# Probabilities times values of the 64 wide heads: three fp32r products of split operands, or one native fp32 product in two column groups of the array

## The chip, the cores and the metric

One NeuronCore of a Trainium2 chip runs the whole program. The metric is the device time of one execution in microseconds (us); lower is better. TensorE (PE in the rows) does matrix products and transposes, VectorE (DVE), ScalarE (ACT) and GpSimd (POOL) the element-wise work, SyncE (SP) issues the DMA transfers. TensorE runs at one of two clock levels, 1.2 or 2.4 GHz; the rows give the granted clock as a share of 2.4 GHz.

## The reference, cut to what matters

The model is two residual layers and a second block, in float32, on 1024 tokens and 256 context tokens of 1024 features. Three of its attentions have heads of 64 features, and only these are touched by the change. Each ends in a product of probabilities and values:

```python
# even layer, windowed heads: 8 heads, 2 of keys and values, 128 queries a block
p = _sink_probs([s_loc, s_ctx], sink).astype(v.dtype)
return (jnp.einsum('bkgqs,bskd->bqkgd', p[..., :span], vn)
        + jnp.einsum('bkgqc,bckd->bqkgd', p[..., span:span + L], vc))
...
# odd layer, neighbourhood heads: 8 heads, 8 rows of the grid and the context
return (jnp.einsum('bhqk,bkhd->bqhd', p[..., :n_loc], vs)
        + jnp.einsum('bhqc,bchd->bqhd', p[..., n_loc:], vc))
...
# second block, dilated heads: 8 heads, causal; three windows, mixed by their denominators
o = jnp.einsum('nbqk,nbkd->nbqd', e, vb) / den[..., None]
```

The other two attentions (differential heads, low-rank heads) have values of 128 features and stay as they are.

## The kernel before, in words

The kernel keeps float32 accuracy with the faster fp32r products by splitting an operand into two fp32r parts, high and low, whose sum is the float32 value. A product of two split operands is three matmuls: high by high, low by high, high by low (lines 236 to 238, `mm3`, for the projections).

The program is a row of stages. In three of them an attention with 64 wide heads is woven with other work: `unit_a` (windowed heads, about 300 to 580 us of the span) with projections, `unit_d` (neighbourhood heads, about 1625 to 1930 us) with gates and half of the output projection, `unit_s` (dilated heads, about 2420 to 2680 us) with gates, a gated unit and half of the output projection. `woven` (line 485) takes steps from two generators so that their TensorE times, as the program notes them, advance in proportion; within an attention `pipe` (line 509) lets later parts of one unit go beside the first parts of the next. Engines run their instructions in program order, so TensorE does what the weave wrote, attention and other work in turns.

A unit has four steps. `front` makes scores of 128 queries (matmuls), their maximum (DVE, line 192), the exponential (ACT) and the division by the denominator (POOL). `back` transposes the probabilities, 128 by 128, on TensorE into a PSUM tile `ps_w`; `pt_evac` (lines 748 to 751) then takes the tile out of PSUM in two: ACT writes the high part, rounded to fp32r, and DVE subtracts it from PSUM to get the low part. The transposed tiles are `a_t`, `d_t` and `d_x` (neighbourhood and context keys), `s_th` and `s_tl`. `end` walks over key tiles of 128 and calls `pv64` (line 871) for each:

```python
    if not first:
        mm(o[0:64, cs], v[:, 0, :], lo, start=False, stop=False)                 # L875
    mm(o[:, cs], v.rearrange("p a e -> p (a e)"), hi, start=first, stop=last)    # L876
    if first:
        mm(o[0:64, cs], v[:, 0, :], lo, start=False, stop=False)                 # L878
```

The values stand in a row as 64 high and 64 low columns. One matmul with 128 stationary columns gives high values by high probabilities in PSUM rows 0 to 63 and low values by high probabilities in rows 64 to 127; a second with 64 columns adds high values by low probabilities. Up to 512 columns stream through, for the windowed heads 4 heads of 128 queries, for the others 4 query tiles of one head; a key tile that only some of the queries see has 384, 256 or 128 columns. `fold` (line 754) adds the two halves: ACT copies rows 64 to 127 out (`fo_a`), DVE adds rows 0 to 63 (`fo_b`), and a DMA writes the rows of y.

The values come from `kv_finish` (windowed) and `v_tok` (the others), which split them (ACT and DVE, lines 198 and 199) and spill 128 columns for a head to DRAM; `vals` loads them for each head.

In all there are 84 calls of `pv64` in the windowed stage (all of 512 columns), 128 in the neighbourhood stage (each of its 16 units: five of 512 columns and one each of 384, 256 and 128) and 96 in the dilated stage (8 units of 512, 384, 256 and 128 columns, 8 units with four of 512 more), 308 in all, and so 616 matmuls.

Another place matters for reading the trace: the state space part of the second block (`ssm`, line 1704) has native fp32 matmuls of 128 rows and 64 columns already, 16 in a row, in turn to PSUM rows 0 to 63 and 64 to 127, and lines 1743 and 1745 have native fp32 matmuls of other shapes.

Of the kernel before, what the change touches and what calls it, by code (L numbers as in the profile page):

```python
# [104 lines left out]
class Kern:  # L105
# [168 lines left out]
class Stream:  # L274
    """split weights one after the other, the next on its way; specs: (src [kc*P, n], how to split or None)"""
# [64 lines left out]
class Slabs:  # L340
    """tiles [k][c] of n columns each, indexed as one [:, k, a:b]"""
# [10 lines left out]
def cols(pair, a, b):  # L352
    """columns a..b of a split operand, by contraction tile"""
# [9 lines left out]
def tlast(n):  # L363
    """groups of tokens, the smaller one first"""
# [3 lines left out]
def cond_silu(K):  # L368
    """silu of c and c_ctx as columns [P, KD, 2]"""
# [419 lines left out]
def unit_a(K, ap, g, n, qd, hd, mask, yd):  # L789
# [1868 lines left out]
```

## Time and profile before

| | |
|---|---|
| device time, median of 3 runs (lowest, highest) | 2860.63 us (2854.64, 2862.84) |
| span of the profiled execution, first to last instruction | 2852.8 us |
| what lies around the span | not listed; the median is 7.8 us above this span |
| PE busy | 2508.2 us, 88% of the span |
| DVE, ACT, POOL busy | 61%, 41%, 30% |
| mean granted clock of TensorE | 0.94 |

The profiled execution's own device time stands in none of the views; the difference of 7.8 us between its span and the median of the runs is taken for what lies around it. A busy PE is no full PE: the ends of matmuls are modelled and overlap the next ones, so how long the engine is taken by one instruction is read from the start of one to the start of the next.

### The profile page before, as it was taken

What the parts mean: (1) busy time and instruction counts of PE and PEld (TensorE: products, weight loads), DVE (VectorE), ACT (ScalarE), POOL (GpSimd) and SP (SyncE); (2) the same over time, 40 slices, a digit from 0 to 9 for tenths busy, and PEclk for the clock granted to TensorE, in tenths of its full rate; (3) what the DMA queues carried; (4) which work ended last, traced back from release to release, by engine and by line L of the source; (5) the groups of instructions that cost most, each with busy time, mean ns of one, the idle gap of its engine ahead of it and who ended that gap; (6) DMA issues with size and microseconds to landing.
All of it is one profiled execution on the core that took longest, in us unless ns stands there. A gap on an engine that the chain in (4) does not pass through costs nothing.

```text
span 2852.8 us, 41862 instructions
## 1 busy us (share of the span) xinstructions
PE 2508.2 (88%) x14199; PEld 2124.0 (74%) x14199; DVE 1747.4 (61%) x5069; ACT 1173.1 (41%) x2589; POOL 868.6 (30%) x1149
## 2 busy tenths in 40 slices
PE   6687889779998977969999899897997889999998
PEld 4567777668977766947988777675996778877777
DVE  7552567557898976434555566668427774667643
ACT  6321455434454533323333355544213332555522
POOL 4231344300034444122232343452013442224410
PEclk9899999889999989989999999999998989999999
DMA  6235433243366443266332454665212224358521
GB/s 224 85 126 165 125 94 86 56 135 111 79 209 208 146 143 127 82 204 244 115 123 100 125 132 113 189 188 174 81 35 61 66 72 151 111 152 249 181 80 44
DMA packets 325496, 370.15 MB, mean 130 GB/s; under 512 B 39596, under 2 KB 258712, under 8 KB 325282
## 3 DMA queue, kind: packets, MB, share of 16 engines
q1 hardware_dynamic: 325122, 367.42, 42.4%
q8 instruction: 113, 1.85, 0.3%
q14 instruction: 101, 0.83, 0.1%
q10 hardware_dynamic: 160, 0.05, 0.0%
HBM read 240.49 MB, written 126.91 MB: 129 GB/s over the span
## 4 chain that ended last, share of the span: by engine, by line
PE 58%; DVE 17%; DMA 14%; POOL 4%; ACT 4%; issue 3%; SPq 1%; DVEq 0%; ACTq 0%; POOLq 0%
PE ps_w L236 11%; PE ps_w L238 10%; PE ps_w L237 10%; PE ps_w L894 4%; PE ps_w L904 3%; PE ps_w L876 2%; PE ps_w L1437 1%; PE ps_w L875 1%; PE ps_s L238 1%; PE ps_s L236 1%; PE ps_s L237 1%; PE ps_w L917 1%; PE ps_w L915 1%; PE ps_w L916 1%; DVE wl L215 1%
## 5 line engine op out<-in xcount | busy, mean ns | idle before, releaser
L215 POOL TENSOR_TENSOR wl<-raw,wh 128x256 fp32r<-128x256 f32 (+1 forms) x266 | 214.5, 822 | 534.2 <-ACT wh L210 384.6
L210 ACT CAST wh<-raw 128x256 fp32r<-128x256 f32 (+1 forms) x430 | 151.6, 402 | 139.3 <-PE ps_w L237 95.1
L215 DVE TENSOR_TENSOR wl<-raw,wh 128x256 fp32r<-128x256 f32 x220 | 128.0, 609 | 123.8 <-ACT wh L210 119.5
L236 PE MATMUL ps_w<-wo_h,o_yh 128*128 128x512 f32 x416 | 177.7, 427 | 15.3 <-ACT o_yh L198 10.1
L236 PE MATMUL ps_w<-e_hh,wh 128*128 128x512 f32 (+1 forms) x480 | 180.9, 377 | 7.0 <-DVE va_t L199 6.7
L238 PE MATMUL ps_w<-wo_h,o_yl 128*128 128x512 f32 x416 | 171.6, 413 | 12.1 <-DVE o_yl L199 12.1
L238 PE MATMUL ps_w<-e_hh,wl 128*128 128x512 f32 (+1 forms) x480 | 174.6, 364 | 5.5 <-DVE wl L215 5.5
L237 PE MATMUL ps_w<-e_hl,wh 128*128 128x512 f32 (+1 forms) x480 | 174.5, 364 | 0.0
L237 PE MATMUL ps_w<-wo_l,o_yh 128*128 128x512 f32 x416 | 170.2, 409 | 0.0
L236 PE MATMUL ps_w<-wh,s_hh 128*128 128x256 f32 x512 | 165.7, 324 | 0.0
L237 PE MATMUL ps_w<-wl,s_hh 128*128 128x256 f32 x512 | 162.7, 318 | 0.0
L238 PE MATMUL ps_w<-wh,s_hl 128*128 128x256 f32 x512 | 162.6, 318 | 0.0
L192 DVE CUSTOM_DVE_ANT_0 b_p<-ps_w,zero 128x512 f32<-128x512 f32 (+1 forms) x192 | 109.5, 593 | 27.8 <-PE ps_w L894 27.6
L236 PE MATMUL ps_w<-o_hh,wh 128*128 128x512 f32 (+1 forms) x288 | 114.9, 399 | 8.1 <-ACT wh L210 7.1
L236 PEld LDWEIGHTS ps_w<-wh,s_hh 128*128 128x128 f32 x512 | 119.5, 233 | 1.8 <-issue 1.1
L237 PEld LDWEIGHTS ps_w<-wl,s_hh 128*128 128x128 f32 x512 | 119.4, 233 | 0.0
L238 PEld LDWEIGHTS ps_w<-wh,s_hl 128*128 128x128 f32 x512 | 119.0, 232 | 0.5 <-issue 0.5
L894 PE MATMUL ps_w<-b_k,b_q 128*128 128x512 f32 (+1 forms) x384 | 95.1, 377 | 25.7 <-DMA b_q<-e_qb 17.0
L238 PE MATMUL ps_w<-o_hh,wl 128*128 128x512 f32 (+1 forms) x288 | 113.1, 393 | 0.6 <-POOL wl L215 0.5
L237 PE MATMUL ps_w<-o_hl,wh 128*128 128x512 f32 (+1 forms) x288 | 113.2, 393 | 0.0
L986 ACT ACTIVATE b_p<-b_p,b_nm 128x1280 f32<-128x1280 f32 x64 | 87.3, 1365 | 59.6 <-DVE b_nm L985 59.3
L236 PEld LDWEIGHTS ps_w<-wo_h,o_yh 128*128 128x128 f32 x416 | 82.8, 199 | 35.5 <-ACT o_yh L198 15.6
(532 smaller groups left out, 7776.2 us busy)
## 6 DMA issues: line engine op xcount, KB each, us to landing
raw<-in_ev_w_ada_dram SPq DMA_DIRECT2D x12, 1024.0 KB
raw<-in_ev_w_in_dram SPq DMA_DIRECT2D x12, 1024.0 KB
raw<-in_od_w_ada_dram SPq DMA_DIRECT2D x12, 1024.0 KB
raw<-in_w_in_dram SPq DMA_DIRECT2D x12, 1024.0 KB
b_k<-e_kb SPq DMA_DIRECT2D x32, 320.0 KB
raw<-in_od_w_in_dram SPq DMA_DIRECT2D x10, 1024.0 KB
d_k<-o_kd SPq DMA_DIRECT2D x32, 320.0 KB
xr<-x SPq DMA_DIRECT2D x16, 512.0 KB
```

Source lines behind the costliest of these rows:

```text
L192: self.nc.vector.tensor_tensor_reduce(out=out, in0=ps, in1=b, scale=1.0, scalar=NEG, op0=ALU.add, op1=ALU.max, accum_out=mx)
L210: nc.scalar.copy(out=h, in_=r)
L215: (nc.vector if b == "D" else nc.gpsimd).tensor_tensor(out=l, in0=r, in1=h.bitcast(F), op=ALU.subtract)
L236: mm(out, ah, bh, start=first, stop=False)
L237: mm(out, ah, bl, start=False, stop=False)
L238: mm(out, al, bh, start=False, stop=last)
L875: mm(o[0:64, cs], v[:, 0, :], lo, start=False, stop=False)
L876: mm(o[:, cs], v.rearrange("p a e -> p (a e)"), hi, start=first, stop=last)
L894: mm(o, q, k[:, ks], start=i == 0, stop=i == n - 1)
L904: K.nc.tensor.transpose(pt[:, i * P:(i + 1) * P], p[:, (j + i) * P:(j + i + 1) * P], K.ident)
L915: mm(o, v[:, 0, :], hi[:, i, :], start=first and i == 0, stop=False)
L986: nc.scalar.activation(out=p, in_=p, func=AF.Exp, bias=nm, accum_out=den)
```

## The change

Only the heads with 64 features are touched. Their values are stored once, as float32 (64 columns a head and not 128), and the transposed probabilities too: ACT copies the PSUM tile out, and the DVE subtraction is gone, as it is from `kv_finish` and from `v_tok` for 64 wide heads. `pv64` now issues native float32 matmuls with the 64 values as stationary columns. The streaming columns are dealt to two column groups of the array: even heads or query tiles go to PSUM rows 0 to 63, odd ones to rows 64 to 127, so that a call with 512 columns becomes two matmuls of 256 columns and `o` is 256 columns wide. `fold` is replaced by `out64`, one ACT copy of 128 by 256 and the DMA; for the neighbourhood and the dilated heads two DMAs, one for each group. The transposed tiles, now one where there were two, have two buffers instead of one; so has `fo_a`. The numbers that steer the weave are the same. (The changed file also drops comments and docstrings, so that line numbers differ: the matmul of `pv64` is its line 894.)

```diff
@@ kv_finish
-        vt = pool.tile([P, 2, 2, 64], FR, tag="va_t", name="va_t", bufs=2)
-        pv = pt[:, 0:128].rearrange("p (f e) -> p f e", f=2)
-        K.split(vt[:, :, 0, :], vt[:, :, 1, :], pv)
-        nc.sync.dma_start(out=vd[t * P:(t + 1) * P, :], in_=vt.bitcast(F).rearrange("p a b e -> p (a b e)"))
+        vt = pool.tile([P, P], F, tag="va_t", name="va_t", bufs=2)
+        nc.scalar.copy(out=vt, in_=pt[:, 0:P])
+        nc.sync.dma_start(out=vd[t * P:(t + 1) * P, :], in_=vt)
@@ v_tok
+        if dv == 64:
+            vt = K.tp.tile([P, n], F, tag="vt%d" % n, name="vt", bufs=K.rb)
+            K.nc.scalar.copy(out=vt, in_=ps[:, :n])
+            K.nc.sync.dma_start(out=vd[t * P:(t + 1) * P, :], in_=vt)
+            yield c
+            continue
@@ fold becomes out64
-def fold(K, ap, o, n, yd, nh):
-    a = ap.tile([64, 512], F, tag="fo_a", name="fo_a", bufs=1)
-    nc.scalar.copy(out=a[:, :n], in_=o[64:128, :n])
-    b = ap.tile([64, 512], F, tag="fo_b", name="fo_b", bufs=1)
-    nc.vector.tensor_tensor(out=b[:, :n], in0=o[0:64, :n], in1=a[:, :n], op=ALU.add)
-    nc.sync.dma_start(out=yd.rearrange("(h p) t -> p h t", p=64), in_=b[:, :n].rearrange("p (h t) -> p h t", h=nh))
+def out64(K, ap, o, dst):
+    a = ap.tile([P, 256], F, tag="fo_a", name="fo_a", bufs=2)
+    nc.scalar.copy(out=a, in_=o)
+    for src, to in dst(a):
+        nc.sync.dma_start(out=to, in_=src.rearrange("p (h t) -> p h t", h=2))
...
+def out_rows(yd):
+    v = yd.rearrange("p (i g t) -> g p i t", g=2, t=P)
+    return lambda a: [(a[g * 64:(g + 1) * 64], v[g]) for g in range(2)]
@@ unit_a, back and end
-        pr = [ap.tile([P, 512], FR, tag="a_t%s%d" % (c, ji), name="a_t", bufs=1) for c in "hl"]
-        pt_evac(K, pt, *pr)
+        pr = ap.tile([P, 4, P], F, tag="a_t%d" % ji, name="a_t", bufs=2)
+        nc.scalar.copy(out=pr, in_=pt.rearrange("p (h t) -> p h t", h=4))
...
-        pv64(K, o, hd["v"][:, js[ji]], pts[ji][0], pts[ji][1], slice(0, 512), ji == 0, ji == nj - 1)
+        pv64(K, o, hd["v"][:, js[ji]], pts[ji], [(0, 4)] * nj, ji)
@@ pv64
-def pv64(K, o, v, hi, lo, cs, first, last):
-    mm = K.nc.tensor.matmul
-    if not first:
-        mm(o[0:64, cs], v[:, 0, :], lo, start=False, stop=False)
-    mm(o[:, cs], v.rearrange("p a e -> p (a e)"), hi, start=first, stop=last)
-    if first:
-        mm(o[0:64, cs], v[:, 0, :], lo, start=False, stop=False)
+def halves(a, b):
+    return [((a - g + 1) // 2, (b - g + 1) // 2) for g in range(2)]
...
+def pv64(K, o, v, p, order, n):
+    for g, (i0, i1) in enumerate(halves(*order[n])):
+        if i1 > i0:
+            end = not any(y > x for x, y in (halves(*r)[g] for r in order[n + 1:]))
+            K.nc.tensor.matmul(o[g * 64:(g + 1) * 64, i0 * P:i1 * P], v, p[:, 2 * i0 + g:2 * i1 + g - 1:2, :], start=n == 0, stop=end)
@@ unit_d, back (unit_s through p_trans in the same way)
-        pt_evac(K, pv.rearrange("p (j t) -> p j t", j=cnt), to[0][:, j:j + cnt, ts], to[1][:, j:j + cnt, ts])
+        nc.scalar.copy(out=to[:, j:j + cnt, i, :], in_=pv.rearrange("p (j t) -> p j t", j=cnt))
```

On TensorE, in the neighbourhood stage, at the end of one unit beside projections of the gates (`o_hh`, `o_hl` by the weights `wh`, `wl`), the kernel before has the `pv64` matmuls on the context keys (`d_x`) and on the first neighbourhood keys (`d_t`) in this order:

```order
L238 MATMUL ps_w<-o_hh,wl_12476 128x512
L875 MATMUL ps_w<-d_x,d_v 64x512
L876 MATMUL ps_w<-d_x,d_v 128x512
L875 MATMUL ps_w<-d_t,d_v 64x384
L876 MATMUL ps_w<-d_t,d_v 128x384
L875 MATMUL ps_w<-d_t,d_v 64x512
L876 MATMUL ps_w<-d_t,d_v 128x512
L236 MATMUL ps_w<-o_hh,wh_12475 128x512
```

At the same end of a unit the changed kernel's TensorE has (L894 is the new `pv64`):

```order
L236 MATMUL ps_w<-o_hh,wh_12257 128x512
L894 MATMUL ps_w<-d_x,d_v 64x256
L237 MATMUL ps_w<-o_hl,wh_12257 128x512
L238 MATMUL ps_w<-o_hh,wl_12258 128x512
L894 MATMUL ps_w<-d_x,d_v 64x256 x2
L894 MATMUL ps_w<-d_t,d_v 64x256
L894 MATMUL ps_w<-d_t,d_v 64x128
L894 MATMUL ps_w<-d_t,d_v 64x256 x2
L236 MATMUL ps_w<-o_hh,wh_12257 128x512
```

The matmuls stand at the same place among the projections; a call's two halves can be parted by other work, as the first row of L894 is here. Counted over the whole order of the changed kernel, the L894 rows form 160 runs without other matmuls between them: 35 in the windowed, 64 in the neighbourhood and 61 in the dilated stage, with 584 matmuls in all, 456 of 256 columns and 128 of 128.

On DVE, in the same stage, right after a split of weights (L215), the kernel before has the fold of the unit before and the low parts of the transposed probabilities:

```order
L215 TENSOR_TENSOR wl_12476<-raw,wh_12475 128x256
L1411 RECIPROCAL d_r<-d_d 128x1
L760 TENSOR_TENSOR fo_b<-ps_w,fo_a 64x512
L751 TENSOR_TENSOR d_t<-ps_w,d_t 128x4x128
L751 TENSOR_TENSOR d_t<-ps_w,d_t 128x128
L751 TENSOR_TENSOR d_t<-ps_w,d_t 128x4x128
L751 TENSOR_TENSOR d_t<-ps_w,d_t 128x128
L751 TENSOR_TENSOR d_x<-ps_w,d_x 128x2x128
L711 SCALAR_TENSOR_TENSOR gth<-gth,ps_w 128x512
```

After the same split the changed kernel's DVE has:

```order
L215 TENSOR_TENSOR wl_12258<-raw,wh_12257 128x256
L192 ISA d_p,d_mx<-ps_s,zero 128x256
L192 ISA d_mx 128x1
L192 ISA d_p,d_mx<-ps_s,d_te 128x512
L192 ISA d_mx 128x1
L1426 TENSOR_REDUCE d_nm<-d_mx 128x1
L1430 RECIPROCAL d_r<-d_d 128x1
L716 SCALAR_TENSOR_TENSOR gth<-gth,ps_w 128x512
```

The `fo_b`, `d_t` and `d_x` rows are gone, and the score maxima of the next query tile (L192) follow at once.

## Rows read from the trace of the kernel before

**Rows 1.** The page: busy time of the engines, and the chain that ended last.
```profile
PE 2508.2 (88%) x14199; PEld 2124.0 (74%) x14199; DVE 1747.4 (61%) x5069; ACT 1173.1 (41%) x2589; POOL 868.6 (30%) x1149
...
PE 58%; DVE 17%; DMA 14%; POOL 4%; ACT 4%; issue 3%; SPq 1%; DVEq 0%; ACTq 0%; POOLq 0%
```
**Rows 2.** Busy time by engine in the three stages, granted clock, DMA share.
```profile
core 0: us, PE busy (x) PEld busy (x) DVE busy (x) ACT busy (x) POOL busy (x), PEclk, DMA share, GB/s
300.00:580.00 280.00, 236.61 (x1324) 200.24 (x1323) 176.26 (x607) 141.56 (x310) 112.89 (x261) 0.91 0.31 85
1625.00:1930.00 305.00, 283.58 (x1467) 223.20 (x1468) 197.39 (x611) 160.77 (x359) 133.11 (x144) 0.95 0.57 153
2420.00:2680.00 260.00, 247.76 (x1263) 199.10 (x1262) 173.76 (x446) 145.52 (x320) 90.25 (x103) 0.97 0.57 174
```
**Rows 3.** Timeline of TensorE, end of a neighbourhood unit: start us, us, instruction.
```profile
1713.74 0.39 PE L875 MATMUL ps_w<-d_t,d_v 128*64 128x512 f32 x1
...
1714.66 0.28 PE L875 MATMUL ps_w<-d_t,d_v 128*64 128x256 f32 x1
...
1714.89 0.40 PE L236 MATMUL ps_w<-o_hh,wh 128*128 128x512 f32 x1
...
1716.29 0.22 PE L875 MATMUL ps_w<-d_t,d_v 128*64 128x128 f32 x1
...
1716.46 0.41 PE L1437 MATMUL ps_w<-ident,d_p 128*128 128x128 f32 x2
```
**Rows 4.** Timeline of TensorE around native fp32 matmuls in two column groups.
```profile
2351.92 0.28 PE L237 MATMUL ps_w<-wl,s_hh 128*128 128x256 f32 x1
2352.20 1.97 PE L1704 MATMUL ps_s<-s_UT,s_BT 128*64 128x128 f32 x32
2354.10 0.39 PE L238 MATMUL ps_w<-wh,s_hl 128*128 128x256 f32 x1
2354.32 0.28 PE L236 MATMUL ps_w<-wh,s_hh 128*128 128x256 f32 x1
2354.44 0.28 PE L237 MATMUL ps_w<-wl,s_hh 128*128 128x256 f32 x1
```
**Rows 5.** Line 1704: weight loads, duration ns min/median/max.
```profile
L1704 PEld LDWEIGHTS ps_s<-s_UT,s_BT x128: 132/137/137, 2137.5 to 2353.8; 128*64 128x64 f32 x128
```
**Rows 6.** Timeline of TensorE: one native fp32 matmul over the full array.
```profile
2200.99 0.38 PE L1743 MATMUL ps_s<-s_TT,s_UT 128*128 128x128 f32 x2
```
**Rows 7.** Costliest DVE groups: busy us, mean ns of one, idle before.
```profile
L751 DVE TENSOR_TENSOR a_t<-ps_w,a_t 128x512 fp32r<-128x512 f32 x84 | 56.9, 684 | 2.3 <-ACT a_t L750 1.7
L751 DVE TENSOR_TENSOR s_tl<-ps_w,s_th 128x512 fp32r<-128x512 f32 (+2 forms) x96 | 52.0, 552 | 13.6 <-ACT s_th L750 13.1
L751 DVE TENSOR_TENSOR d_t<-ps_w,d_t 128x512 fp32r<-128x512 f32 x96 | 50.7, 551 | 10.9 <-ACT d_t L750 10.7
L760 DVE TENSOR_TENSOR fo_b<-ps_w,fo_a 64x512 f32<-64x512 f32 x52 | 35.4, 681 | 70.7 <-ACT fo_a L758 58.2 <-DMA e_y<-fo_b 12.3
L751 DVE TENSOR_TENSOR d_x<-ps_w,d_x 128x256 fp32r<-128x256 f32 x64 | 26.4, 418 | 4.7 <-ACT d_x L750 4.2
```
**Rows 8.** What TensorE waited for: us in total, times, longest us.
```profile
PE ps_s L1390 <- DVE d_mx L192: 8.4, 6, 5.5
PE ps_w L236 <- DVE va_t L199: 6.7, 1, 6.7
PE ps_w L876 <- DVE fo_b L760: 6.2, 1, 6.2
PE ps_s L1845 <- DVE s_mx L192: 3.6, 3, 1.5
PE ps_w L1437 <- DVE d_t L751: 2.5, 6, 0.8
PE ps_w L875 <- DVE a_t L751: 2.0, 2, 1.7
```
**Rows 9.** Busy time by engine, 15 us of the state space part.
```profile
2176.00:2191.00 15.00, 13.81 (x53) 11.47 (x54) 6.46 (x25) 4.96 (x8) 2.09 (x2) 0.50 0.52 145
```

More of the change, by code (lines that the diff above doesn't have):

```diff
@@ L777, in vals @@
         def vals():
-            hd["v"] = ap.tile([P, 10, 2, 64], FR, tag="a_v", name="a_v", bufs=K.kb)
-            nc.sync.dma_start(out=hd["v"].bitcast(F).rearrange("p j a e -> p j (a e)"), in_=vd.rearrange("(j p) (g e) -> p j g e", p=P, g=2)[:, :, g, :])
+            hd["v"] = ap.tile([P, 10, 64], F, tag="a_v", name="a_v", bufs=K.kb)
+            nc.sync.dma_start(out=hd["v"], in_=vd.rearrange("(j p) (g e) -> p j g e", p=P, g=2)[:, :, g, :])
         for n in range(10):
@@ L904, in p_trans @@
         K.nc.tensor.transpose(pt[:, i * P:(i + 1) * P], p[:, (j + i) * P:(j + i + 1) * P], K.ident)
+    if len(pt_) == 1:
+        K.nc.scalar.copy(out=pt_[0][:, :, off:off + P], in_=pt[:, :c * P].rearrange("p (j t) -> p j t", j=c))
+        return 0.107 * c
+    hi, lo = pt_
     pt_evac(K, pt[:, :c * P].rearrange("p (j t) -> p j t", j=c), hi[:, :, off:off + P], lo[:, :, off:off + P])
@@ L1418, in back @@
         if i == 0 and k == 0:
-            dst.append([dp.tile([P, 6, 512], FR, tag="d_t" + c, name="d_t", bufs=1) for c in "hl"])
-            dst.append([dp.tile([P, 2, 512], FR, tag="d_x" + c, name="d_x", bufs=1) for c in "hl"])
+            dst.append(dp.tile([P, 6, 4, P], F, tag="d_t", name="d_t", bufs=2))
+            dst.append(dp.tile([P, 2, 4, P], F, tag="d_x", name="d_x", bufs=2))
         loc, ctx = dst
@@ L1454, in end @@
         src, st, j, a, b = order[oi]
-        cs = slice(a * P, b * P)
-        pv64(K, S_["o"], hd["v"][:, j], src[0][:, st, cs], src[1][:, st, cs], cs, oi == 0, oi == 7)
+        pv64(K, S_["o"], hd["v"][:, j], src[:, st], [x[3:] for x in order], oi)
         if oi == 7:
             assert len(order) == 8
-            fold(K, dp, S_["o"], 512, yd, 1)
+            out64(K, dp, S_["o"], out_rows(yd))
         return 0.2 * (b - a)
@@ L1818, in vals @@
         def vals():
[L1819 to L1820 removed]
+            hd["v"] = sp.tile([P, 8, 64], F, tag="s_v", name="s_v", bufs=1)
+            nc.sync.dma_start(out=hd["v"], in_=vd[h // 4].rearrange("(j p) (h e) -> p j h e", p=P, h=4)[:, :, h % 4, :])
         for half in range(2):
@@ L1860, in back @@
         if len(pts) <= g:
-            pts.append(pt_tile(K, sp, "s_t", 512, g, 4, (4, 4)))
+            pts.append(sp.tile([P, 4, 512], F, tag="s_t%d" % g, name="s_t", bufs=2))
         n = half * 4 + i
         c = min(4, n + 1 - g * 4)
-        return p_trans(K, ps[i], g * 4, [t[:, 0:c, :] for t in pts[g]], i * P, c)
+        return p_trans(K, ps[i], g * 4, [pts[g][:, 0:c, :]], i * P, c)
     os = []
@@ L1869, in end @@
         if j == 0:
-            os.append(K.w())
+            os.append(K.w()[:, 0:256])
         nj = half * 4 + 4
-        cs = slice(max(0, j - half * 4) * P, 512)
-        hi, lo = pts[j // 4]
-        pv64(K, os[0], hd["v"][:, j], hi[:, j % 4, cs], lo[:, j % 4, cs], cs, j == 0, j == nj - 1)
+        p = pts[j // 4][:, j % 4].rearrange("p (i t) -> p i t", i=4)
+        pv64(K, os[0], hd["v"][:, j], p, [(max(0, x - half * 4), 4) for x in range(nj)], j)
         if j == nj - 1:
-            fold(K, sp, os[0], 512, yd, 1)
+            out64(K, sp, os[0], out_rows(yd))
         return 0.3
@@ L2293, in stages @@
     kd = [K.dram([2, 2, 64, T], "o_kd%d" % i) for i in range(4)]
-    vd = [K.dram([T, 512], "o_vd%d" % i) for i in range(2)]
+    vd = [K.dram([T, 256], "o_vd%d" % i) for i in range(2)]
     sg = [K.dram([512, S], "o_sg%d" % i) for i in range(2)]
@@ L2472, in stages @@
     nm = Norm(K, jk)
-    vd = [K.dram([S, 512], "s_vd%d" % i) for i in range(2)]
+    vd = [K.dram([S, 256], "s_vd%d" % i) for i in range(2)]
     K.tp, K.rb = jk, 2
```

17 lines of the change are left out of this document (7 added, 10 removed).

## The prediction

> **What bounds the kernel now.** I read the page first: PE is busy 88% of the span and carries 58% of the chain that ended last, DVE 17% of it [rows 1]. The average says little about the three stages that the change touches, so I then took the windows of these stages [rows 2]. PE is idle there for 280 - 236.6 = 43.4 us, 305 - 283.6 = 21.4 us and 260 - 247.8 = 12.2 us, 77.0 us of 845 in all. DVE is busy 63%, 65% and 67%, so it has a third of its time free. The granted clock of TensorE is 0.91, 0.95 and 0.97; against a full clock this loses about 0.09 x 280 + 0.05 x 305 + 0.03 x 260 = 25 + 15 + 8 = 48 us. The reader is to see that PE is the engine with the least room in the neighbourhood and the dilated stage, and has some room in the windowed one. What lengthens PE's work therefore counts nearly in full; what shortens DVE's counts only where PE stood waiting for DVE, and for those places I read the list of PE's waits [rows 8].
>
> **What PE pays now for probabilities times values.** From start to start, two calls of 512 columns take 1714.66 - 1713.74 = 0.92 us, so one (two matmuls) takes 0.46; one of 256 columns takes 0.23, one of 128 columns 0.17 [rows 3]; for 384 I take the middle, 0.35. The stationary operand changes between 64 and 128 columns within these calls, and no time is lost over it. With the counts of calls by width: windowed 84 x 0.46 = 38.6 us; neighbourhood 16 x (5 x 0.46 + 0.35 + 0.23 + 0.17) = 48.8; dilated 8 x (0.46 + 0.75) + 8 x (5 x 0.46 + 0.75) = 34.1. Sum: 121.5 us.
>
> **What PE pays after.** The trace of before has the same kind of matmul: line 1704, native fp32, 128 rows by 64 columns, in turn to the two halves of PSUM [rows 4]. 16 products show as 32 records, so each is two passes. One native product over the full array takes two records in 0.38 us [rows 6], and a matmul's record is 0.28 long where its slot is 0.12 [rows 4], so I read a pass of 128 columns there as 0.38 - 0.28 = 0.10 to 0.11 us, two cycles a column at 2.4 GHz. Around line 1704: the slot of L237 ends at 2351.92 + 0.12 = 2352.04, that of L238 begins at 2354.32 - 0.12 = 2354.20, so 2.16 us lie between. 32 passes of 0.109 one after the other would be 3.5 us; side by side in two groups they are 1.74. So the groups do run at the same time, and 2.16 - 1.74 = 0.42 us are left over, which go to entering and leaving the divided array: L1704 starts only when L237's record has ended (2352.20), and L238 has a record of 0.39 instead of 0.28. So a visit costs 0.42 us beside its passes.
>
> A matmul of 256 columns is then 2 x 0.217 = 0.43 us, one of 128 columns 0.22. All 584 in a row would be 456 x 0.43 + 128 x 0.22 = 224 us; perfectly paired, 112. They aren't perfectly paired: a call with an odd number of tiles, or a run with one matmul, leaves a group empty. Taking for each of the 160 runs of the order the fuller of its two groups gives 36 us (windowed, 35 runs), 54 (neighbourhood, 64 runs) and 35 (dilated, 61 runs), 126 in all. The passes alone thus cost what the three split products cost before, 126 against 121.5. What is new is 160 visits x 0.42 = 67 us. The sum on PE: 126 + 67 - 121.5 = +72 us, of it 13 windowed, 32 neighbourhood, 27 dilated. Bounds for a visit: 0 us if PE would have been idle there anyhow, 0.84 at the lower clock level. Some visits will fall in idle time (77 of 845 us), some at the lower level (clock 0.91 to 0.97); the two weigh about the same, so I keep 0.42.
>
> The page "TensorEngine Tiling (Array Packing)" of the Trainium skill (Key Properties) says that a change of the tiling mode, not merely of the tile, drains TensorE. The row above shows that for native fp32. Were narrow fp32r matmuls a mode of their own too, the kernel before would drain some 600 times now and the change would gain more than 100 us; the starts in rows 3 exclude it.
>
> **What the other engines save.** DVE loses the low parts (56.9 + 52.0 + 50.7 + 26.4 us) and the fold (35.4), 221 us of busy time [rows 7], and smaller subtractions for the values. ACT's work stays, one copy for a tile. None of this is time of the kernel by itself. What PE waited for at operations that vanish is 6.7 (`va_t`), 6.2 (`fo_b`, whose single buffer waited for its DMA), 2.5 (`d_t`) and 2.0 (`a_t`) [rows 8], 17.4 us; I take all of it, since ACT's copy, which remains, stood ahead of each before as well. What PE waited for at score maxima, which queue behind the low parts on DVE, is 8.4 and 3.6; I take half, 6. Idle time also lowers the clock: these 17 us within the stages (23.4 less the 6.7 of `va_t`) are 22% of the idle 77, so I give back 22% of the 48 us lost to the clock, 10. Sum: 33 us. Bounds: 0, if the waits only move to the next late thing (`d_p` of POOL, the DMA of keys), and 77 + 48 + 7 = 132, if all idle time and all clock loss of the stages went.
>
> **At no cost.** The value loads carry half of the bytes, the added 32 output DMAs (two for one, 16 units twice) are issued by SP long before the y rows are read, and the second buffers free nothing that PE is seen to wait for. If the y rows came late, the first projection of the next part would wait once a stage, by a few us.
>
> **Sum.** The profile's span of 2852.8 and the 7.8 us up to the median make 2860.6; +72 - 33 = +39, so 2900 us.
>
> **Rivals.** *DVE gives back more than PE pays.* On the other side: the three stages would be held by the chain scores, maximum, exponential, transposes, evacuation, in which DVE comes twice, and with 221 us less on DVE the idle time and the clock come back. For it: the waits at DVE in rows 8 and the lower clock of the windowed stage. Against: PE's idle time in the other two is 34 us. It decides once more than 72 us come back out of the 132; with three quarters (99) the time is 2834. *It balances*: 64 to 80 us come back, 2860. *The clock falls further.* With PE drained 160 times, more stretches go to the lower level. For it: in the state space part, where native products of different array shapes alternate (lines 1743, 1745), the engine was busy 13.8 of 15 us and yet at 0.50 [rows 9]. Against: line 1704's visits ran at the full level. If the clock loss of the stages doubles, +48: 2948. *The groups don't run side by side*, as accumulation in one bank could have it: 224 instead of 126, 2998. Rows 4 speak against, which share all but the accumulation. *Weight loads come into the open.* Each of the 1168 passes has its own load of 64 columns, 0.137 us [rows 5]; two side by side, uncovered, are 584 x 0.137 = 80 us: 2980. Rows 4 speak against: 32 loads fit in the 2.16 us. The Trainium skill's page "TensorE: Matmul & The Clock Gate" (Part 3, What overlaps and what doesn't) has such a rule: loads overlap matmuls in flight only if the row group differs, which here it doesn't; this trace does not bear it out.
>
> **How the numbers follow.** Chances: my forecast 0.62 (2870 to 2925), more than DVE's relief 0.12, balance 0.08, lower clock 0.12, no pairing 0.03, open loads 0.03. About 0.3% (8.6 us) is what a measurement of this kernel can tell from no change. Faster 0.12, same 0.08, slower 0.80. The range holds the forecast, the balance and the lower clock, 0.82: 2855 to 2950.
>
> **What would show it.** Right, if in the changed trace L894's passes of 256 columns start in twos, 0.22 us apart, each run begins after the record before it has ended, and the next full matmul's record is some 0.1 us longer; if PE's instructions have fewer idle us in the three stages, DVE's busy time is lower by some 220 us, and the neighbourhood and dilated stages are each longer by 15 to 30 us, the windowed one by little. Wrong, if the passes come one by one, if the windows show a clock under 0.90, or if the stages became shorter because idle time of PE nearly vanished.

## The result, and the profile of the changed kernel

The changed kernel takes 2893.4 us in the median of 4 runs (2890.4 to 2902.8); the kernel before 2861.7 (4 runs, 2854.6 to 2863.2). The ratio is 1.0123, with an interval of 1.0103 to 1.0142, so it is slower by 32 us by the medians and 35 by the ratio. The prediction was 2900, in a range of 2855 to 2950, with 0.80 for slower.

The page of the changed kernel, busy time of the engines and the chain that ended last, answers to [rows 1]:

```profile
PE 2555.1 (88%) x14751; PEld 2104.6 (73%) x14751; DVE 1543.5 (53%) x4631; ACT 1154.7 (40%) x2589; POOL 867.8 (30%) x1149
...
PE 61%; DVE 14%; DMA 13%; POOL 4%; issue 3%; ACT 3%; SPq 1%; DVEq 0%; ACTq 0%; POOLq 0%
```

DVE has 1747.4 - 1543.5 = 204 us less to do, and the kernel is slower nevertheless. The windows of the three stages (the later two have moved back and grown, so their borders are moved too) answer to [rows 2]:

```profile
core 0: us, PE busy (x) PEld busy (x) DVE busy (x) ACT busy (x) POOL busy (x), PEclk, DMA share, GB/s
300.00:580.00 280.00, 240.11 (x1481) 189.29 (x1480) 119.66 (x503) 135.19 (x310) 111.71 (x260) 0.93 0.28 82
1625.00:1950.00 325.00, 301.85 (x1691) 215.36 (x1692) 117.56 (x435) 154.73 (x360) 132.58 (x143) 0.96 0.53 137
2445.00:2710.00 265.00, 257.43 (x1384) 183.39 (x1383) 115.38 (x325) 137.54 (x314) 85.55 (x100) 0.98 0.52 156
```

DVE is busy 43%, 36% and 44% of the stages instead of 63 to 67%. PE's idle time is 39.9, 23.1 and 7.6 us, not much less than the 43.4, 21.4 and 12.2 of before. The clock is a little higher.

The timeline of TensorE shows the new products in the windowed stage (start us, us, instruction; two records for a matmul), beside [rows 3] and [rows 4]:

```profile
314.18 0.40 PE L822 MATMUL ps_w<-a_k,a_q 128*128 128x256 f32 x2
314.51 1.08 PE L894 MATMUL ps_w<-a_t,a_v 128*64 128x256 f32 x8
315.52 0.50 PE L236 MATMUL ps_w<-e_hh,wh 128*128 128x512 f32 x1
```

Eight passes of 256 columns, one after the other, would be 8 x 0.217 = 1.73 us; the next instruction starts after 315.52 - 314.51 = 1.01. The groups run side by side. L894 starts 0.33 us after L822 (a slot of 0.23), and L236's record is 0.50 long where its usual one is 0.39.

What TensorE waits for in the windowed stage (us, times, longest) answers to [rows 8]:

```profile
PE ps_w L819 <- DMA a_k<-e_ka: 13.5, 1, 13.5
PE ps_w L819 <- DMA a_q<-e_qa: 9.1, 3, 4.7
PE ps_w L822 <- DVE rlo L621: 6.7, 1, 6.7
PE ps_w L822 <- DMA a_q<-e_qa: 3.5, 1, 3.5
PE ps_w L822 <- ACT a_t L848: 3.2, 2, 2.7
```

The same list for the neighbourhood stage:

```profile
PE ps_s L1409 <- DVE d_mx L192: 9.0, 8, 4.8
PE ps_w L1455 <- POOL d_p L1432: 7.0, 7, 2.2
PE ps_s L1409 <- DMA d_q<-o_qd: 3.7, 1, 3.7
```

The waits for `fo_b` and for DVE's `a_t` and `d_t` are gone. The waits for the maxima `d_mx` haven't become shorter (9.0 for 8.4), and in the windowed stage TensorE now waits 26.1 us for loads of `a_k` and `a_q`, where it waited 15.3 before. The same list for the windowed stage of the kernel before:

```profile
PE ps_w L812 <- DVE rlo L621: 13.6, 2, 8.0
PE ps_w L809 <- DMA a_k<-e_ka: 11.0, 1, 11.0
...
PE ps_w L809 <- DMA a_q<-e_qa: 4.3, 2, 3.0
```

For the whole comparison I split each stage, from its first score to the end of its last product of probabilities and values, into four parts: its length; TensorE's idle time (the waits of all its instructions, added up); the clock loss (half of the time at the lower level in which it wasn't idle); and the rest, which is TensorE's work at full clock. The same was done for every experiment below (us):

| kernel | windowed: length, idle, clock, work | neighbourhood | dilated | sum |
|---|---|---|---|---|
| before | 270.5, 45.1, 13.5, 211.9 | 298.4, 27.5, 13.6, 257.3 | 244.2, 11.5, 5.5, 227.2 | 813.1, 84.1, 32.6, 696.4 |
| changed | 272.0, 41.9, 12.2, 218.0 | 317.2, 27.6, 10.0, 279.5 | 258.7, 7.6, 4.6, 246.5 | 848.0, 77.0, 26.9, 744.1 |
| e_gather | 267.1, 40.0, 13.6, 213.6 | 305.3, 32.2, 10.2, 262.9 | 242.9, 9.2, 6.1, 227.6 | 815.3, 81.3, 29.8, 704.1 |
| e_gather_late | 263.0, 38.1, 11.4, 213.5 | 307.9, 36.2, 15.1, 256.6 | 244.0, 10.0, 6.2, 227.8 | 814.9, 84.2, 32.7, 697.9 |
| e_full | 287.8, 32.4, 10.4, 245.1 | 326.1, 23.4, 5.7, 297.0 | 265.9, 9.0, 4.3, 252.6 | 879.8, 64.8, 20.4, 794.7 |
| e_relief | 274.0, 47.9, 15.6, 210.5 | 301.3, 30.4, 12.8, 258.1 | 242.4, 9.7, 6.9, 225.8 | 817.8, 88.0, 35.3, 694.4 |
| e_dve_back | 258.5, 31.9, 7.9, 218.7 | 314.0, 28.9, 10.2, 274.8 | 260.3, 9.2, 3.8, 247.3 | 832.8, 70.0, 21.9, 740.8 |
| e_loads | 253.7, 25.4, 10.3, 218.0 | 347.4, 48.6, 23.8, 275.0 | 259.7, 8.4, 4.7, 246.6 | 860.7, 82.5, 38.7, 739.5 |
| e_loads_before | 265.0, 42.1, 9.8, 213.1 | 325.4, 49.6, 22.7, 253.2 | 245.7, 12.9, 4.7, 228.2 | 836.2, 104.6, 37.1, 694.5 |
| e_loads_late | 250.1, 29.3, 7.0, 213.7 | 316.8, 41.5, 20.3, 254.9 | 245.1, 9.7, 7.5, 228.0 | 812.0, 80.5, 34.9, 696.6 |
| e_loads_a | 253.5, 26.2, 10.4, 216.9 | 316.3, 28.6, 7.3, 280.4 | 258.6, 7.6, 4.7, 246.3 | 828.3, 62.4, 22.3, 743.6 |
| e_loads_a_before | 264.8, 41.1, 10.7, 213.0 | 294.3, 26.1, 9.2, 259.0 | 244.3, 10.7, 6.7, 227.0 | 803.4, 77.8, 26.6, 698.9 |
| e_relief_loads_a | 263.1, 41.1, 13.0, 209.1 | 302.1, 31.0, 13.2, 257.9 | 242.8, 9.9, 7.0, 225.8 | 808.0, 82.0, 33.1, 692.9 |
| e_best | 250.9, 30.7, 8.4, 211.8 | 309.6, 32.4, 15.0, 262.1 | 242.7, 9.2, 5.8, 227.8 | 803.2, 72.3, 29.2, 701.7 |

So the change adds 744.1 - 696.4 = 47.7 us of work to TensorE, and gets back 7.1 of idle time and 5.7 of clock: +34.9 in the stages. Another 4.0 us are added between the neighbourhood and the dilated stage (5.2 up to the first projection of the second block, of which 1.2 come back), and 2.0 after the dilated stage. From span to span it is +40.4 (2893.2 - 2852.8); the medians differ by 32, since the profiled execution of before was one of its shorter ones: where a run is listed with its span, some 2 us lie around the span (2895.2 for 2893.2), so the span of 2852.8 is the run of 2854.6, and what lies around it isn't the 7.8 us that stand ahead of the prediction. Each row of the table is one execution; those of before, e_loads_before and e_loads_a_before lie 6 to 8 us under their medians, that of e_loads 7 above, the others within 5. So a few us between two rows tell nothing by themselves.

### The profile page after: what moved, and what is told of

The parts are those of the page before. It is cut to its first block, busy times and chain, and to the rows that moved or that the text cites. A ratio compares the mean times of both kernels' runs of the same rounds, so it can differ in the third digit from the quotient of the medians.

```text
span 2893.2 us, 42402 instructions
## 1 busy us (share of the span) xinstructions
PE 2555.1 (88%) x14751; PEld 2104.6 (73%) x14751; DVE 1543.5 (53%) x4631; ACT 1154.7 (40%) x2589; POOL 867.8 (30%) x1149
## 4 chain that ended last, share of the span: by engine, by line
PE 61%; DVE 14%; DMA 13%; POOL 4%; issue 3%; ACT 3%; SPq 1%; DVEq 0%; ACTq 0%; POOLq 0%
PE ps_w L236 11%; PE ps_w L238 10%; PE ps_w L237 10%; PE ps_w L910 5%; PE ps_w L894 5%; PE ps_w L919 3%; PE ps_w L1455 1%; DMA a_q<-e_qa 1%; PE ps_w L934 1%; DMA e_vb<-vt 1%; PE ps_w L936 1%; PE ps_w L935 1%; PE ps_s L238 1%; PE ps_s L236 1%; PE ps_s L237 1%
## 5 line engine op out<-in xcount | busy, mean ns | idle before, releaser
L215 POOL TENSOR_TENSOR wl<-raw,wh 128x256 fp32r<-128x256 f32 (+1 forms) x266 | 214.3, 821 | 543.6 <-ACT wh L210 396.6
L215 DVE TENSOR_TENSOR wl<-raw,wh 128x256 fp32r<-128x256 f32 x220 | 125.9, 599 | 167.2 <-ACT wh L210 153.9
L236 PE MATMUL ps_w<-wo_h,o_yh 128*128 128x512 f32 x416 | 177.7, 427 | 15.7 <-ACT o_yh L198 11.6
L236 PE MATMUL ps_w<-e_hh,wh 128*128 128x512 f32 (+1 forms) x480 | 182.8, 381 | 2.3 <-ACT wh L210 2.1
L238 PE MATMUL ps_w<-wo_h,o_yl 128*128 128x512 f32 x416 | 169.6, 408 | 12.0 <-DVE o_yl L199 12.0
L238 PE MATMUL ps_w<-e_hh,wl 128*128 128x512 f32 (+1 forms) x480 | 175.0, 365 | 5.4 <-DVE wl L215 5.3
L237 PE MATMUL ps_w<-e_hl,wh 128*128 128x512 f32 (+1 forms) x480 | 174.5, 364 | 0.0
L237 PE MATMUL ps_w<-wo_l,o_yh 128*128 128x512 f32 x416 | 168.5, 405 | 0.0
L236 PE MATMUL ps_w<-wh,s_hh 128*128 128x256 f32 x512 | 167.0, 326 | 0.0
L237 PE MATMUL ps_w<-wl,s_hh 128*128 128x256 f32 x512 | 164.1, 321 | 0.0
L238 PE MATMUL ps_w<-wh,s_hl 128*128 128x256 f32 x512 | 164.0, 320 | 0.0
L236 PE MATMUL ps_w<-o_hh,wh 128*128 128x512 f32 (+1 forms) x288 | 117.3, 407 | 6.8 <-ACT wh L210 6.4
L192 DVE CUSTOM_DVE_ANT_0 b_p<-ps_w,zero 128x512 f32<-128x512 f32 (+1 forms) x192 | 109.6, 594 | 25.7 <-PE ps_w L910 25.6
L236 PEld LDWEIGHTS ps_w<-wh,s_hh 128*128 128x128 f32 x512 | 120.8, 236 | 1.6 <-issue 1.1
L238 PEld LDWEIGHTS ps_w<-wh,s_hl 128*128 128x128 f32 x512 | 120.4, 235 | 0.5 <-issue 0.5
L237 PEld LDWEIGHTS ps_w<-wl,s_hh 128*128 128x128 f32 x512 | 120.6, 236 | 0.0
L238 PE MATMUL ps_w<-o_hh,wl 128*128 128x512 f32 (+1 forms) x288 | 113.0, 392 | 0.6 <-POOL wl L215 0.5
L237 PE MATMUL ps_w<-o_hl,wh 128*128 128x512 f32 (+1 forms) x288 | 113.4, 394 | 0.0
L236 PEld LDWEIGHTS ps_w<-wo_h,o_yh 128*128 128x128 f32 x416 | 81.2, 195 | 43.4 <-ACT o_yh L198 16.2
```

The costliest lines, as they stand in the source:

```text
L192: self.nc.vector.tensor_tensor_reduce(out=out, in0=ps, in1=b, scale=1.0, scalar=NEG, op0=ALU.add, op1=ALU.max, accum_out=mx)
L215: (nc.vector if b == "D" else nc.gpsimd).tensor_tensor(out=l, in0=r, in1=h.bitcast(F), op=ALU.subtract)
L236: mm(out, ah, bh, start=first, stop=False)
L237: mm(out, ah, bl, start=False, stop=False)
L238: mm(out, al, bh, start=False, stop=last)
```

## The experiments

### What entering and leaving the divided array costs

My theory: each visit of the divided array costs TensorE 0.42 us beside its passes. The rival: the visits fall into idle time, and the added time is elsewhere. Two kernels gather all native calls of a unit into one step of the weave:

```diff
+def at_once(f, n):
+    return [lambda: sum(f(i) for i in range(n))]
...
-    return [[load], each(front, 4), each(back, nj), whole(end, nj)]
+    return [[load], each(front, 4), each(back, nj), at_once(end, nj)]         # e_gather; unit_d, unit_s alike
+    return [[load], each(front, 4), each(back, nj), None, at_once(end, nj)]   # e_gather_late; unit_d, unit_s alike
```

> The changed kernel, with all the native calls of one unit written as one step of the weave, so that they stand in 65 runs on TensorE (20 windowed, 28 neighbourhood, 17 dilated) and not in 160 (35, 64, 61). Matmuls, bytes and work of the other engines are the same. Theory (each entry and exit of the divided array costs TensorE 0.42 us): 95 visits fewer are 40 us, and fuller groups in the longer runs give a few more, 44 in all: 2893 - 44 = 2850, at least 2840 to 2865; the neighbourhood and dilated stages are each some 15 to 20 us shorter than with the change as given. Rival A (the added time is in the passes themselves, or in what the other engines do, and the visits fall where TensorE is idle anyhow): no change, 2885 to 2900. Rival B (steps in one piece hold the scores back, and DVE and ACT then come late): longer than 2900, with new waits for the transposed probabilities.

> As the kernel with gathered calls, and the gathered step stands one step of the pipe later, beside the first parts of the next unit, so that the last transposed tile and its copy are long done when it begins: 61 runs (20, 23, 18). Theory: 2846, so 0 to 8 us under the kernel that gathers without the shift; what it takes off beyond the 4 runs are waits for ACT's copies ahead of the gathered calls. Rival A (visits cost nothing): 2885 to 2900. Rival B (a wait for the copies bound the gathered calls): more than 10 us under the kernel that gathers without the shift.

Measured: 2867.6 us (1.0034 of before, 1.0013 to 1.0055) and 2864.5 us (1.0017, 1.0004 to 1.0031). Gathering takes off 26 of the 32 us that the change cost, though not the 44 of the theory, and the time lies just outside its range; the first rival falls, and with it the one that the scores would be held back. TensorE's work falls by 744.1 - 704.1 = 40.0 us for 95 visits fewer. That the time falls by less has its place in the table: idle time and clock loss of the stages grow by 4.3 and 2.9, and the stretches between and after them lose the rest. With the shift, TensorE's work is at 697.9, level with before, but the neighbourhood stage gains 4.0 of idle time and 4.9 of clock loss (one wait of 9.6 us for `d_q`), so little is won.

A long run shows a visit in its parts; the timeline of TensorE in e_gather, windowed stage:

```profile
330.40 0.40 PE L238 MATMUL ps_w<-e_hh,wl 128*128 128x512 f32 x1
330.73 2.38 PE L898 MATMUL ps_w<-a_t,a_v 128*64 128x256 f32 x20
333.04 0.50 PE L236 MATMUL ps_w<-e_hh,wh 128*128 128x512 f32 x1
```

L238 has a slot of 0.23 us and L898 starts after 0.33: 0.10 for entering. Twenty passes in two groups are 10 x 0.217 = 2.17, and L236 starts after 2.31: 0.14 between. L236's record is 0.50 instead of 0.39: 0.11 for leaving. In all 0.35 us a visit. Over the visits of the changed kernel at full clock without a wait in them the median of the remainder is 0.34 us for runs of one, two, four and eight matmuls of 256 columns alike (13, 18, 25 and 2 runs; single ones from 0.29 to 0.44), so it doesn't hang on the length. The slots of the native products themselves add up to 149.8 us at full clock in the changed kernel and to 131.0 in e_gather: 18.8 less, 95 x 0.14 = 13 of them from within the visits and the other 5 or 6 from fuller groups. With 95 x 0.21 = 20 for entering and leaving, 39 of the 40 us are found.

The same products without a divided array, over 128 columns:

```diff
-            hd["v"] = ap.tile([P, 10, 64], F, tag="a_v", name="a_v", bufs=K.kb)
+            hd["v"] = ap.tile([P, 10, 2, 64], F, tag="a_v", name="a_v", bufs=K.kb)   # loaded twice
...
-            K.nc.tensor.matmul(o[g * 64:(g + 1) * 64, i0 * P:i1 * P], v, p[:, 2 * i0 + g:2 * i1 + g - 1:2, :], start=n == 0, stop=end)
+    K.nc.tensor.matmul(o[:, a * P:b * P], v.rearrange("p a e -> p (a e)"), p[:, a:b, :], start=n == 0, stop=n == len(order) - 1)
```

> The native fp32 products over the full array: the values stand twice side by side as 128 stationary columns, a call streams 512 columns at once, there are no column groups and no divided array; ACT copies PSUM rows 0 to 63 out. No visits, but passes one after the other, 224 us by 0.109 us for 128 columns of a pass. Theory A, by the numbers of the prediction (126 of passes and 67 of visits in the changed kernel): 224 - 193 = +31 on the changed kernel, 2924. Theory B, by what gathering gave (0.27 us a visit, so 126 + 43 = 169): +55, 2948. Rival (the two groups don't in fact run side by side, and the changed kernel pays 224 and the visits): 2850.

Measured: 2926.0 us (1.0243, 1.0206 to 1.0280). The rival, groups that don't run side by side, falls. The time fits theory A, but not by its way: TensorE's work is 794.7 - 744.1 = 50.6 us above the changed kernel, nearer to theory B's 55, and 19 us of that come back, 12.2 of idle time and 6.5 of clock loss. In the windowed stage, with SP's order at 390 us as in the changed kernel, it waits 18.8 us for `a_k` and `a_q` and not 26.1; a longer TensorE seems to meet the same late loads later. Against before the work is +98.3. From the passes alone 224 - 125.3 = 98.7 are expected, with 125.3 us for the old calls as their slots in the trace of before add up at full clock. So native fp32 products among fp32r ones pay no visit as long as the array isn't divided; the price is that of the two groups.

### What DVE's relief gives

My theory: of the 33 us, 15 to 25 come from DVE's low parts alone. The rivals: DVE's work was hidden, or held the stages. One kernel takes the low parts out of before, another puts their work back into the changed kernel:

```diff
# e_relief, on before (unit_d and unit_s alike)
-        pr = [ap.tile([P, 512], FR, tag="a_t%s%d" % (c, ji), name="a_t", bufs=1) for c in "hl"]
-        pt_evac(K, pt, *pr)
+        pr = [ap.tile([P, 512], FR, tag="a_th%d" % ji, name="a_t", bufs=1)] * 2
+        nc.scalar.copy(out=pr[0], in_=pt)
# e_dve_back, on the changed kernel (unit_d and unit_s alike)
+        low = ap.tile([P, 4, P], F, tag="a_low", name="a_low", bufs=1)
+        nc.vector.tensor_tensor(out=low, in0=pt.rearrange("p (h t) -> p h t", h=4), in1=pr, op=ALU.subtract)
```

> The kernel before, in which DVE no longer makes the low parts of the 64 wide heads' probabilities; the second matmul of each call takes the high part again, so the output leaves the low part out. TensorE's instructions, the fold and the split of the values stay. It measures what DVE's relief gives by itself. Theory (the waits for low parts vanish and those at the maxima halve; the wait for the fold stays): 15 to 25 us less than before, about 2840. Rival A (DVE's time is hidden, the waits only move): 2855 to 2862. Rival B (DVE holds the stages): 2800 or less; then TensorE's added work in the change is over 90 us, more than its prediction says.

> The changed kernel, with a DVE subtraction added behind each copy of the transposed probabilities, from PSUM into a tile that nothing reads (the work of the old low parts, without the fold and without a reader on TensorE). Theory (relief at the maxima and in the release of the PSUM tiles is 15 to 20 us of the 33): 2905 to 2915. Rival A (all relief came from readers that no longer wait for DVE, not from DVE's own queue): 2890 to 2897. Rival B (relief was far larger than 33): 2930 or more.

Measured: 2867.6 us for e_relief (1.0035, 1.0021 to 1.0048), 8 us more than before; 2878.2 us for e_dve_back (1.0072, 1.0057 to 1.0087), 15 us less than the changed kernel. Both have the sign opposite to my theory, and no rival had it either: here less work on DVE went with a longer kernel, more work with a shorter one. My theory of the relief falls. Relief there is all the same, and most of it doesn't hang on the time of DVE's low parts: e_dve_back, with 163 us of DVE's work put back, has 14.1 us less idle time and 10.7 less clock loss in the stages than before. It keeps of the change, among other things, that no reader waits for the fold or for a low part.

The table shows where the 15 us are: e_dve_back is 13.5 us shorter than the changed kernel in the windowed stage, with 10.0 less idle time. Its waits there:

```profile
PE ps_w L822 <- DVE rlo L621: 11.8, 2, 6.5
PE ps_w L819 <- DMA a_k<-e_ka: 10.5, 1, 10.5
PE ps_w L819 <- DMA a_q<-e_qa: 4.1, 3, 1.5
```

The loads of `a_k` and `a_q` hold it for 14.6 us and not for 26.1. So I read SP's queue in the timeline (start us, us, instruction; L642 stores parts of the projections, L810 loads `a_q`). The changed kernel:

```profile
388.95 1.10 SPq L642 DMA_DIRECT2D e_kb<-rhi  x2
390.21 1.71 SPq L642 DMA_DIRECT2D e_kb<-rlo  x2
392.00 2.83 SPq L810 DMA_DIRECT2D a_q<-e_qa  x1
```

The same place in e_dve_back:

```profile
386.10 1.10 SPq L642 DMA_DIRECT2D e_kb<-rhi  x2
387.31 0.47 SPq L810 DMA_DIRECT2D a_q<-e_qa  x1
387.88 4.13 SPq L642 DMA_DIRECT2D e_kb<-rlo  x2
```

And in the kernel before, where L800 loads `a_q`:

```profile
386.71 1.13 SPq L642 DMA_DIRECT2D e_kb<-rhi  x2
387.94 0.46 SPq L800 DMA_DIRECT2D a_q<-e_qa  x1
388.50 4.14 SPq L642 DMA_DIRECT2D e_kb<-rlo  x2
```

Without the low parts on DVE, the order written for SP has the store of `rlo` ahead of the query load (e_relief has it so too, with the load at 395.83 us); with them it has the load first. The change never names these instructions. In the changed kernel the load is issued some 4 us later than before, at 392.00, behind both stores, and TensorE is idle for `a_q` for 3.5 us at 405.3, which neither of the other two shows. Another place follows: at 443.46 us a store of y comes, for which SP had waited 12.2 us for `fo_a`, then the stores of `e_qb`, and only at 446.35 the next loads of `a_q`, for which TensorE is idle for 4.7 us at 453.6. In e_dve_back these loads are issued at 435.27, in before at 435.97.

### The loads taken off SP's queue

The new theory: late loads of the windowed heads ate the relief. To test it, ACT issues them:

```diff
-                    nc.sync.dma_start(out=hd["k"][j].bitcast(F)[d * 64:(d + 1) * 64, :], in_=kd[g, j])
+                    nc.scalar.dma_start(out=hd["k"][j].bitcast(F)[d * 64:(d + 1) * 64, :], in_=kd[g, j])
-        nc.sync.dma_start(out=qs[0].bitcast(F), in_=qd[g].rearrange("h a d t -> (a d) h t")[:, :, n * P:(n + 1) * P])
+        nc.scalar.dma_start(out=qs[0].bitcast(F), in_=qd[g].rearrange("h a d t -> (a d) h t")[:, :, n * P:(n + 1) * P])
```

At first the neighbourhood heads' loads of `d_q` and `d_k` were moved in the same way, on three kernels:

> The changed kernel, with the loads of queries and keys of the windowed and the neighbourhood heads issued by ACT and not by SP; nothing else. Theory (without DVE's low parts the stores of the projections' low parts stand ahead of the query loads in SP's order, at about 390 us and 835 us, and the scores wait for late loads): of the 26.1 us that TensorE waits for a_q and a_k in the windowed stage of the changed kernel at least 10 vanish, and with them some half-clock time, 12 us in all there, and 4 in the neighbourhood stage: 2877, 2870 to 2885. Rival A (the loads are late for what they themselves wait for, the release of their tiles or the projections): 2890 to 2896. Rival B (issuing holds ACT back, its copies of transposed tiles come late): over 2900.

> The kernel before with the same move of the loads to ACT, as the control. Theory (its SP order has the loads ahead already; only the key load in the middle of the windowed stage, 11 us, is left to gain): 0 to 8 us less than before, 2852 to 2860. Rival (the loads on SP are late in general, not by the change's order): 15 or more less, 2845 or lower.

> The kernel with gathered native calls one step later, with the same move of the loads to ACT. Its neighbourhood stage has a wait of 9.6 us for d_q and 8.1 us for d_k, its windowed stage 25.1 for a_q and a_k. Theory: half of these 43 us and some clock come back, 20 to 25 us: 2840 to 2845, which is less than the kernel before. Rival A: the waits move to the next late thing, 2860 to 2866. Rival B: ACT late, over 2870.

Measured: 2909.0 (1.0176, 1.0146 to 1.0205), 2893.7 (1.0116, 1.0087 to 1.0145) and 2868.6 us (1.0030, 1.0015 to 1.0045). All three miss; e_loads comes out in the range of its rival B, but the list below shows waits for the loads themselves and not for ACT's copies of transposed tiles. The theory holds in the windowed stage, which falls to 253.7 us, 265.0 and 250.1; the neighbourhood stage rises to 347.4, 325.4 and 316.8. What TensorE waits for there in e_loads:

```profile
PE ps_s L1409 <- DMA d_q<-o_qd: 18.9, 4, 6.5
PE ps_s L1409 <- DMA d_k<-o_kd: 7.9, 3, 4.5
PE ps_s L1409 <- issue: 7.5, 3, 5.0
```

The queries of these heads (`d_q`) have a single buffer, so their load must stand behind the scores that still read it; on ACT it also stands among the exponentials of these scores. That this is the cause was not tested by itself. So the move was undone for the neighbourhood heads:

> The changed kernel with only the windowed heads' loads of queries and keys issued by ACT; the neighbourhood heads' stay on SP. With both moved the windowed stage went from 272.0 to 253.7 us and the neighbourhood stage from 317.2 to 347.4. Theory: the gain of the windowed stage stays, 18 us: 2875, 2870 to 2880. Rival (the gain is given back by the next stages, whose projections the weave places beside the windowed stage): 2888 or more.

> The kernel before with only the windowed heads' loads issued by ACT, as the control of the other three. Theory (windowed stage 270.5 to 265.0 when both were moved): 5 us less than before, 2855; rival: no change, or all of the changed kernel's gain of 18.

> The kernel before without DVE's low parts of the 64 wide heads' probabilities (the second matmul takes the high part again, so the output leaves the low part out), with the windowed heads' loads issued by ACT. Theory (DVE's relief was eaten by query loads that came to stand behind stores in SP's order, 274.0 us for the windowed stage against 270.5): that stage falls to about 260, and the time to 2850 to 2855, no more than the control. Rival (the relief costs by something else): 5 us or more above the control, 2860 to 2866.

> The changed kernel with the native calls of a unit gathered in one step (in the windowed heads one step later), and with the windowed heads' loads issued by ACT. By the stages of the kernels so far: windowed 250, neighbourhood 305, dilated 243, so 20 us under before in the first, 7 over it in the second, 1 under in the third, and 10 over in the stretches after them: 2850 to 2857, under before and level with the control. Rival (the gains don't add, since earlier stages only start later ones earlier against the same loads): 2863 to 2868.

Measured: e_loads_a 2874.0 us (1.0048, 1.0034 to 1.0062), 19 less than the changed kernel and as the theory had it; its control e_loads_a_before 2860.7 (0.9999, 0.9986 to 1.0012), no change, as its rival had it, although its windowed stage is 5.7 us shorter in the profile; e_relief_loads_a 2862.3 (1.0006, 0.9993 to 1.0019), 5 less than e_relief and level with the control, where the theory had wanted it at 2855 or less; e_best 2856.5 (0.9980, 0.9969 to 0.9992), within its theory's range. The waits of e_loads_a in the windowed stage:

```profile
PE ps_w L822 <- DVE rlo L621: 7.6, 2, 6.0
PE ps_w L819 <- DMA a_k<-e_ka: 6.0, 1, 6.0
PE ps_w L894 <- DVE rlo L621: 3.9, 1, 3.9
PE ps_w L819 <- DMA a_q<-e_qa: 3.6, 1, 3.6
```

26.1 us of waits for loads have become 9.6. And in the control, e_loads_a_before:

```profile
PE ps_w L812 <- DVE rlo L621: 18.9, 3, 9.6
...
PE ps_w L809 <- DMA a_k<-e_ka: 6.0, 1, 6.0
...
PE ps_w L809 <- DMA a_q<-e_qa: 1.5, 1, 1.5
```

The same two lines of code are worth 19 us in the changed kernel and nothing that can be told in the kernel before. That the change cost the loads their place is shown by SP's order, and TensorE's waits for loads had grown by 26.1 - 15.3 = 10.8 us. That this is all of the 19 is not shown: in the control, too, 15.3 us of waits for loads become 7.5, but there the waits for DVE's `rlo` grow from 13.6 to 18.9. So a part of the 19 can be late loads that the kernel before has as well, and that its busier DVE hides. Nor is the one store ahead of the one load the whole of it: e_gather_late has the load ahead of both stores (at 388.75 us) and still waits 25.1 us for loads, 16.7 of it for `a_k`. And e_relief_loads_a says that DVE's low parts, with the loads out of the way, are worth nothing that can be told.

e_best (gathered, windowed calls a step later, windowed loads on ACT) is 37 us faster than the changed kernel and 3 us under before, which is less than the 0.3% that can be told from no change. No version here beats both kernels by more.

## Why the prediction was right, and where its terms were off

The sum came out: +39 predicted, +32 by the medians. TensorE's side is the mechanism named, passes that cost about what they did and visits on top; gathering shows it. But both terms were too large, PE's by 24 us and the relief by 20, and that these nearly cancel is luck. One step, the loads at no cost, failed.

**What PE pays: +72 predicted, +47.7 measured.** By stage 13, 32 and 27 were predicted, and 6.1, 22.2 and 19.3 came. The old calls were right (121.5; their slots in the trace of before add up to 125.3 at full clock), and the pairing of the passes too (L894's slots are 149.8 us, and 126 with 160 x 0.14 within the visits make 148). 126 of passes and 160 visits at 0.34 make 180, less 125.3 is +55. The mis-sized factor is the visit, 0.42 us read from the one place at line 1704 [rows 4], where 0.34 was measured: 54 us and not 67. Most of the difference is at the entry: L1704 began 0.16 us after the slot before it, when L237's record had ended; L894 begins 0.10 after it, at 314.51, and so 0.07 before the end of L822's record. The last 7 us between 55 and 47.7 lie outside the slots of the native products and were not traced; they are 1% of the work in the table.

**What the other engines save: -33 predicted, -12.8 measured in the stages.** This term was made of parts that didn't behave alike. The waits for the fold and for DVE's `a_t` vanished and stayed away, 12.2 us in the windowed stage, where 10.8 of new waits for loads took their place. The 6.7 us of `va_t` (at 152 us) gave nothing: the first score of the windowed stage starts at 297.9 us, 298.0 before. The wait moved to the next late thing, the splits of weights (`wh`, `wl`): for these TensorE waits 21.2 us between 160 and 250 us, 15.6 before. The half that I took of the waits at the maxima didn't come (8.4 and 3.6 before, 9.0 and 3.1 after). With the loads out of the way the term is nearer to its size: from before to e_loads_a idle time falls by 21.7 us and clock loss by 10.3, 32 together; measured against the control with the same loads it is 15.4 and 4.3. What failed is the assumption that the waits at the maxima shrink when DVE has less to do: in e_relief, with 155 us less on DVE (1592.0 for 1747.4), the waits at the maxima are 9.2 and 4.6.

**At no cost.** This step failed, and the sum doesn't show it, since the visits were overrated by 13 us. I had counted the bytes of the loads and the added output DMAs, and not asked whether other instructions of SP change places. They did: waits for loads grew by 10.8 us in the windowed stage, and e_loads_a, with these loads off SP, gets 19 us back, of which the changed order is a part. The sentence on late y rows fits better: in the stretch after the neighbourhood stage 5.2 us are added, with waits for `o_yh` of 3.56 and `o_yl` of 4.52 where before had 0.75 and 1.93. But e_relief, which still stores with one DMA a unit, adds 4.0 there as well, by one wait of 7.7 us for DVE (`xu`), and e_full, which also stores with one DMA, adds nothing; what holds the y rows stays open.

**The rivals.** That the groups don't run side by side falls with the starts at 314.51 and with e_full. That weight loads come into the open falls too, in the trace of the changed kernel itself:

```profile
L894 PEld LDWEIGHTS ps_w<-a_t,a_v x336: 132/137/232, 314.5 to 569.4; 128*64 128x64 f32 x168
314.51 0.63 PEld L894 LDWEIGHTS ps_w<-a_t,a_v 128*64 128x64 f32 x8
```

A load takes 0.137 us, and two passes start every 0.217, so two loads one after the other would not fit. But the eight loads of the visit at 314.51 stand in 0.63 us, where one after the other they would take 1.10, and while its passes run (until 315.52): the loads of a pair run side by side, under the passes. The Trainium skill's rule on loads and row groups (page "TensorE: Matmul & The Clock Gate", Part 3, What overlaps and what doesn't) would have them uncovered in one row group, and this trace does not agree. The rule that a change of the mode drains the engine ("TensorEngine Tiling (Array Packing)", Key Properties) agrees, with 0.34 us as the price here. That the clock falls further didn't come: 0.93, 0.96 and 0.98 in the windows. That DVE gives back more than PE pays falls with the table, 12.8 us for 47.7.

**The signs.** The passes start in twos, 0.22 us apart, and the next full matmul's record is 0.11 us longer, as forecast; that a run begins only after the record before it has ended is not so. DVE's busy time fell by 204 us and not by 220. The neighbourhood and the dilated stage are longer by 18.8 and 14.5 us and the windowed one by 1.5, as forecast or nearly; idle time fell in the windowed and the dilated stage and not in the neighbourhood stage (27.6 for 27.5).

## What to carry to other kernels

Count the visits, not only the passes: a short native product in column groups among full fp32r products paid 0.34 us each time it came, and gathering the calls of a unit gave back 26 of 32 us. Work taken off an engine is worth only the waits of the others that end sooner by it, and two experiments, one that takes it away from the old kernel and one that puts it back into the new one, say so quickly. And compare the order on the DMA queue too, for instructions that the diff doesn't name: where an order is worked out from what the other engines have to do, a load can lose its place, as the query load at 390 us did.

## What the runs showed of the hardware that I had not expected

A visit has three parts at full clock: 0.10 us later start, 0.14 within, and 0.11 on the first full matmul behind it, whose record is 0.50 and not 0.39 us long; in the median it is the same for runs of 1 to 10 matmuls. Native fp32 products over the full array pay none of it (e_full, +98.3 us of work for 98.7 of passes). Matmuls of 64 stationary columns in fp32r, between ones of 128, pay none of it [rows 3].

In three kernels idle time shrinks where TensorE's own work grows: from 84.1 us with 696.4 of work to 77.0 with 744.1 and 64.8 with 794.7, and clock loss from 32.6 to 26.9 and 20.4. So 98.3 us of work in e_full cost 66.7 in the stages. It is no rule: e_loads_a has 62.4 us of idle time with 743.6 of work.
